# Softmax sums spread by two 64-column products, twelve key rows throughout, and two head pairs prepared between projections

## The chip, the cores and the metric

The kernel runs on one core of one Trainium2 chip. The metric is device time in microseconds (us); the kernel before takes 3126.86 us, the median of three runs (3126.22 to 3132.38). Less is better.

## What is computed

A two-layer backbone works on 1024 latent tokens (a grid of 16 rows by 64 columns) and 256 context tokens, 1024 channels wide, in float32. Each layer has a modulated norm, one input projection that feeds three parallel mixers (mLSTM, neighbourhood attention, RG-LRU), an output projection with a gated residual, and an MLP. The change touches the attention mixer of 8 heads of 64 channels:

```python
q, k = rmsnorm(q.reshape(sh), qn_g), rmsnorm(k.reshape(sh), kn_g)
...
s_loc = einsum('bqhd,brqchd->bhqrc', q_r, k_win) * scale      # a window of 8 rows x 16 columns of keys
s_loc = s_loc + bias                                          # relative-position table
s_ctx = einsum('bqhd,bkhd->bhqk', q_r, kc) * scale            # 256 context keys
p = softmax(concatenate([s_loc, s_ctx], axis=-1), axis=-1)
o = einsum(p_loc, v_win) + einsum(p_ctx, vc)
```

In the first layer the 256 context queries attend to the context as well; in the last layer they are left out.

## The kernel before, in words

**Precision.** Weights and activations are split into two float32r parts, so that each projection is three TensorE products (L436, L451, L1325, L1477). Score products use stacks [hi; lo] of q against [hi; hi] and [lo; lo] of k.

**Order.** The program is written as one trace; a list scheduler orders each engine's in-order queue by a simulated timeline and, among what is ready there, by the order in the program. So an instruction that stands late in the program can be put early when the simulation has its inputs and its buffer ready, and a queue then waits at that place until they really are.

**Stages around the change, in each layer.** `na_group(0)` and `na_group(1)` (L610) project k, q and v of heads 0 to 3 and 4 to 7, token tile by token tile (`proj_tm`, 24 products a tile in alternating PSUM banks p and q), and spill them to DRAM. `na_prep(hp)` (L625) prepares one pair of heads from that spill in 6 steps (5 in the last layer): load `ut` (L642), scale by the norm on VectorE (L645), transpose up to 4 tiles on TensorE (L653, L655), split into hi and lo on ScalarE and VectorE (L661, L662, L666, L667), copy across partitions by DMA (L669, L672, L673). Pairs 0 and 1 need only group 0. Before, pair 0 is written after `na_group(1)` (L1285), and pair hp+1 step by step inside the attention of pair hp, through `side()` (L1373). `side()` also issues steps of the output projection (`fill`, L1345), whose product bank is one bank p with an evacuation on VectorE (L1342). In layer 0 the projections also share TensorE with pending modulation steps (L266, L274), which load 512 KB of weights each.

**Attention of a pair** (`na_att`, L726). A unit is 8 rows x 16 columns of queries of both heads: 8 latent units a pair, and 2 context units a pair in layer 0 (72 units in all). Scores go to bank a (L795 for the window, L799 for the context), VectorE adds the table `tab` and takes the minimum (L809, L813), ScalarE exponentiates and sums into `den` (L816). `softmax_pv` (L676) transposes the scores (L688), copies them to SBUF (`PT`: L690, L705 on ScalarE, L707 on VectorE), inverts `den` (L710), copies it out to 64 columns a head (`rb`, L712), transposes that (L714) into the upper half of bank c, and multiplies by the values (L718) into the lower half. `yd` then copies and scales the result (L826, L827). Units of query group g = 0 use 11 key rows (352 keys, so that the third key tile has 96), those of g = 1 use 12. The tables of a column tile are loaded (L769) and get one GpSimd addition of a prepared mask tile `crm` (L772). `crm` is made once a layer (L1368, L1371).

**Memory.** The pool `ns` (stacks, `ut`, `ql`) opens before `na_group(1)` in space that the mLSTM leaves; the pool `na_` (npl: scores, `PT`, `rb`, `VC`, `tab`, `VB`, `crm`) opens after it, when the normalised input is closed.

Of the kernel before, what the change touches and what calls it, by code (L numbers as in the profile page):

```python
# [21 lines left out]
P = 128  # L22
# [11 lines left out]
# column offsets inside the combined input projection  # L34
# [4 lines left out]
# token blocks: (offset, size, is_context)  # L39
# [3 lines left out]
def host_consts():  # L43
    """Arrays that depend on shapes alone."""
# [19 lines left out]
    # column mask: partitions (h, ic'), [3 column types, 32 key columns]  # L64
# [8 lines left out]
    # row mask: partitions (i', ic'), [group slot (1, 0), 12 key rows]  # L73
# [18 lines left out]
def backbone_kernel(ctx: ExitStack, tc: tile.TileContext, I, out, dbg=None):  # L92
# [9 lines left out]
    # the normalised blocks lie on one side, all else on the other; they change sides after each attention  # L102
# [62 lines left out]
    def rsqrt(x, tmp_i, tmp_z, y):  # L165
        """y = 1/sqrt(x) for positive x, to float32 accuracy (integer seed and Newton steps)."""
# [7 lines left out]
    def rsqrt_mean(ss, n, inv, tag):  # L174
        """1/sqrt(ss * inv + EPS) of a [P, n] tile of sums."""
# [29 lines left out]
    def w_fm(w, l, c0, r0=0, kt=KT, cols=P):  # L205
        """Weight tile [P, kt, cols] of rows r0.. and columns c0.. of layer l."""
# [41 lines left out]
    # c_act, cctx_act: 32 columns per k tile (two used)  # L248
# [69 lines left out]
    def mod_sum(l, j, ns):  # L318
        """Sums over the partitions of the products of ns steps."""
# [1237 lines left out]
```

## Time and profile before

| | |
|---|---|
| three runs, us | 3132.38, 3126.86, 3126.22 |
| span of the profiled execution, us | 3122.6 |
| PE busy | 3016.5 us, 97% of the span |
| DVE busy | 1898.7 us, 61% |
| ACT busy | 1129.1 us, 36% |
| POOL busy | 288.9 us, 9% |
| mean granted TensorE clock, of 2.4 GHz | 0.989 |

The span runs from the first to the last instruction of one execution taken by the profiler; the page prints no other time of that execution. The three runs lie 3.6 to 9.8 us above the span. PE is TensorE's products, PEld its weight loads, DVE VectorE, ACT ScalarE, POOL GpSimd, SP the queue that issues most transfers. A busy PE is not a PE at its peak, since ends of products are modelled. The granted clock has two levels, 1.2 and 2.4 GHz; a window's figure is the mean share of 2.4 GHz.

### The profile page before, as it was taken

Reading aid. Unit: us, or ns where it says so; the run is one execution under the profiler, and the core shown is the slowest. Engines: PE = TensorE matmul, PEld = TensorE weight load, DVE = VectorE, ACT = ScalarE, POOL = GpSimd, SP = SyncE. Lnnn points to the kernel's source line nnn. Section 1 sums busy time; section 2 is a strip of 40 time slices with the busy share of each in tenths; the row PEclk is TensorE's granted clock in tenths of the full one; section 3 lists DMA queues with packets and bytes.
Section 4 is the critical chain, followed back from the end, with each engine's and each line's share of the span. In section 5 each row is a group of like instructions: output and inputs, shape, how many; then the busy total and the mean of one; then the engine's idle time right before and its main releaser. Section 6 shows DMA issues by size and latency. Waiting matters only on the chain.

```text
span 3122.6 us, 47473 instructions
## 1 busy us (share of the span) xinstructions
PE 3016.5 (97%) x18250; PEld 2553.0 (82%) x18250; DVE 1898.7 (61%) x4318; ACT 1129.1 (36%) x2011; POOL 288.9 (9%) x252
## 2 busy tenths in 40 slices
PE   7999998999899999999999999998899999999999
PEld 6888887878788888887778889997787777887877
DVE  5757654887887666455444584755787444444444
ACT  4632223674422222233222453234564223332222
POOL 0410010122200000010000511002222000000000
PEclk9999999999899999999999999999999999999999
DMA  9624667865233444233333532348753332343333
GB/s 272 223 73 124 174 172 206 234 186 176 67 109 109 123 127 124 79 108 99 92 94 95 176 122 82 101 123 222 223 169 113 95 95 88 99 117 90 93 96 93
DMA packets 531098, 410.73 MB, mean 132 GB/s; under 512 B 27580, under 2 KB 496536, under 8 KB 530872
## 3 DMA queue, kind: packets, MB, share of 16 engines
q1 hardware_dynamic: 519448, 387.41, 42.1%
q0 software_dynamic: 8576, 15.00, 1.5%
q10 hardware_dynamic: 2848, 5.28, 0.6%
q8 instruction: 144, 2.36, 0.3%
q14 instruction: 82, 0.67, 0.1%
HBM read 339.72 MB, written 67.53 MB: 130 GB/s over the span
## 4 chain that ended last, share of the span: by engine, by line
PE 70%; DVE 11%; DMA 10%; issue 2%; ACT 2%; SPq 1%; POOL 0%; ACTq 0%; DVEq 0%; POOLq 0%
PE psa L436 15%; PE psa L1477 14%; PE psq L436 5%; PE psp L436 5%; PE psp L1477 5%; PE psq L1477 5%; PE psp L451 4%; DMA mr<-in_w_mod_dram 4%; PE psq L451 4%; PE psp L1325 2%; DVE ma L312 2%; PE psc L718 2%; DVE wl L201 1%; PE psa L1325 1%; PE psb L688 1%
## 5 line engine op out<-in xcount | busy, mean ns | idle before, releaser
L200 ACT ACTIVATE wh<-wr 128x1024 fp32r<-128x1024 f32 (+3 forms) x356 | 361.6, 1021 | 946.5 <-PE psa L1477 307.3
L201 DVE TENSOR_TENSOR wl<-wr,wh 128x1024 fp32r<-128x1024 f32 (+3 forms) x356 | 425.0, 1198 | 386.4 <-ACT wh L200 380.0
L436 PE MATMUL psa<-xlo,wh 128*128 128x512 f32 (+1 forms) x856 | 319.7, 374 | 2.2 <-DVE xlo L412 2.2
L436 PE MATMUL psa<-xh,wh 128*128 128x512 f32 (+1 forms) x856 | 319.4, 373 | 2.4 <-ACT xh L411 2.3
L436 PE MATMUL psa<-xh,wl 128*128 128x512 f32 (+1 forms) x856 | 319.6, 373 | 1.4 <-DVE wl L201 1.4
L1477 PE MATMUL psa<-hl,wh 128*128 128x512 f32 (+1 forms) x768 | 286.0, 373 | 0.6 <-DVE hl L211 0.6
L1477 PE MATMUL psa<-hh,wh 128*128 128x512 f32 (+1 forms) x768 | 284.2, 375 | 0.3 <-ACT wh L200 0.3
L1477 PE MATMUL psa<-hh,wl 128*128 128x512 f32 (+1 forms) x768 | 277.9, 373 | 0.6 <-DVE wl L201 0.6
L1481 DVE SCALAR_TENSOR_TENSOR res<-psa,modt,res 128x512 f32<-128x512 f32 (+1 forms) x192 | 131.0, 693 | 170.3 <-PE psa L1477 169.9
L436 PEld LDWEIGHTS psa<-xh,wh 128*128 128x128 f32 x856 | 162.1, 190 | 33.4 <-ACT xh L411 3.1
L436 PEld LDWEIGHTS psa<-xlo,wh 128*128 128x128 f32 x856 | 162.1, 189 | 33.1 <-DVE xlo L412 2.6
L436 PEld LDWEIGHTS psa<-xh,wl 128*128 128x128 f32 x856 | 162.1, 189 | 32.3 <-DVE wl L201 2.2
L377 POOL TENSOR_TENSOR acc<-acc,nsq 128x512 f32<-128x512 f32 (+1 forms) x56 | 77.9, 1401 | 1026.9 <-ACT nsq L376 976.5
L1477 PEld LDWEIGHTS psa<-hh,wh 128*128 128x128 f32 x768 | 144.3, 188 | 34.6 <-ACT wh L200 8.6
L451 PE MATMUL psp<-wl,xh 128*128 128x256 f32 (+1 forms) x560 | 164.0, 293 | 4.3 <-DVE wl L201 4.2
L1477 PEld LDWEIGHTS psa<-hh,wl 128*128 128x128 f32 x768 | 144.3, 188 | 28.7 <-DVE wl L201 1.5
L1477 PEld LDWEIGHTS psa<-hl,wh 128*128 128x128 f32 x768 | 144.4, 188 | 27.4 <-DVE hl L211 0.8
L210 ACT ACTIVATE hh<-rl 128x512 fp32r<-128x512 f32 (+1 forms) x160 | 93.5, 589 | 202.1 <-DVE rl L1453 202.0
L451 PE MATMUL psp<-wh,xh 128*128 128x256 f32 (+1 forms) x560 | 161.9, 289 | 2.4 <-ACT wh L200 2.4
L451 PE MATMUL psq<-wh,xh 128*128 128x256 f32 (+1 forms) x560 | 161.7, 289 | 1.4 <-ACT usq L605 0.9
L451 PE MATMUL psq<-wl,xh 128*128 128x256 f32 (+1 forms) x560 | 160.6, 287 | 0.0
L451 PE MATMUL psp<-wh,xlo 128*128 128x256 f32 (+1 forms) x560 | 159.9, 286 | 0.0
(409 smaller groups left out, 7328.5 us busy)
## 6 DMA issues: line engine op xcount, KB each, us to landing
wr<-in_w_mlp_dram SPq DMA_DIRECT2D x256, 512.0 KB
mr<-in_w_mod_dram SPq DMA_DIRECT2D x92, 512.0 KB
wr<-in_w_in_dram SPq DMA_DIRECT2D x48, 512.0 KB
tab<-T_d SPq DMA_DIRECT2D x48, 384.0 KB
T_d<-E_d POOLq DMA_DIRECT2D x48, 256.0 KB, 6.6
ab<-row_d SPq DMA_DIRECT2D x36, 256.0 KB
xT_d<-res SPq DMA_DIRECT2D x4, 2048.0 KB
wr<-in_w_out_dram SPq DMA_DIRECT2D x32, 256.0 KB
```

What stands on the lines that cost most here:

```text
L200: act.activation(hi[:, a:b], raw[:, a:b], AF.Copy)
L201: dve.tensor_sub(lo[:, a:b], raw[:, a:b], hi[:, a:b].bitcast(F32))
L210: act.activation(hi, src32, AF.Copy)
L312: dve.scalar_tensor_tensor(a, raw[:, k], s[:, k], a, op0=OP.mult, op1=OP.add)
L377: pool.tensor_add(acc[bi], acc[bi], sq[:, :n])
L436: m = pe.matmul(t[:, :n], w[a][:, k, :], X[bi][b][:, k, :], start=(i == 0), stop=(i == 23))
L451: pe.matmul(t[:, :cols], X[bi][b][:, half * 4 + k, o:o + P], ws[half][a][:, k, :], start=(i == 0), stop=(i == 23))
L688: pe.transpose(t[:w, j * P:(j + 1) * P], S[e][:, o:o + w], permT)
L718: pe.matmul(to[64 * e:64 * e + 64, :P], vals[i][:w, 64 * e:64 * e + 64], PT[:w, e, i], start=(i == 0), stop=(i == nt - 1))
L1325: pe.matmul(t[:, :n], w[a][:, k, cc * P:(cc + 1) * P], Y[bi][b][:, k], start=(i == 0), stop=(i == 11))
L1477: m = pe.matmul(t[:, :n], w[a][:, k, cc * P:(cc + 1) * P], H[bi, k][b], start=(i == 0), stop=(i == 3 * GH - 1))
L1481: dve.scalar_tensor_tensor(xr[bi][:, ct], t[:, :n], G2[:, ct, v:v + 1], xr[bi][:, ct], op0=OP.mult, op1=OP.add)
```

## The change

`softmax_pv` no longer copies `den` to 64 columns and transposes it; for each head one product takes `den` itself, read 64 times, as a 64-column stationary operand against the permutation. All units use 12 key rows, so all key tiles have 128 keys and `PT` is copied in whole pieces. `crm` is dropped: each table gets two GpSimd additions with masks read repeatedly. `VC` and `tab` move from pool npl to `ns`. Steps of the first two pairs' preparation are written after every second token tile of `na_group(1)`, until 12 (10 in the last layer) have been issued, and both are completed there; `side()` prepares only pairs 2 and 3, beside the attention of pairs 1 and 2. What else the diff changes is comments.

```diff
-        def na_proj(grp, c0, dst, toks, stat):
+        def na_proj(grp, c0, dst, toks, stat, side):
...
+                if side is not None:
+                    side()
             proj_tm(ws, 256, X, toks, ev)
...
-                    t = bank("b" if hp < 1 else "bbq")
+                    t = bank("b" if hp < 2 else "bbq")
...
-                    o, w = tiles[i]
-                    pe.transpose(t[:w, j * P:(j + 1) * P], S[e][:, o:o + w], permT)
+                    pe.transpose(t[:, j * P:(j + 1) * P], S[e][:, tiles[i]:tiles[i] + P], permT)
...
-                while j < 4:
...
-                    if e == 0:
-                        act.activation(PT[:w, e, j:j2], src, AF.Copy)
-                    else:
-                        dve.tensor_copy(PT[:w, e, j:j2], src)
-                    j = j2
+                elif gi == 0:
+                    act.activation(PT[:, 0, 0:4], t.rearrange("p (k q) -> p k q", q=P), AF.Copy)
+                else:
+                    dve.tensor_copy(PT[:, 1, 0:4], t.rearrange("p (k q) -> p k q", q=P))
             dve.reciprocal(den, den)
-            rb_ = npl.tile([P, 2, 64], F32, name=nm("rb"), tag="rb", bufs=2)
-            dve.tensor_copy(rb_, den.unsqueeze(2).to_broadcast([P, 2, 64]))
             to = bank("c")
-            pe.transpose(to[:, P:2 * P], rb_.rearrange("p e d -> p (e d)"), permT)
+            for e in range(2):
+                pe.matmul(to[64 * e:64 * e + 64, P:2 * P], den[:, e:e + 1].to_broadcast([P, 64]), permT,
+                          start=True, stop=True)
...
-            VC = npl.tile([P, 2, P], F32, name=nm("VC"), tag="VC", bufs=1)
+            VC = ns.tile([P, 2, P], F32, name=nm("VC"), tag="VC", bufs=1)
...
-                    tb_ = npl.tile([P, 2, 384], F32, name=nm("tab"), tag="tab", bufs=4)
+                    tb_ = ns.tile([P, 2, 384], F32, name=nm("tab"), tag="tab", bufs=4)
...
-                    pool.tensor_add(tv, tv, crm[ct].rearrange("p (r c) -> p r c", c=32))
+                    pool.tensor_add(tv, tv, masks[:, 96:120].unsqueeze(2).to_broadcast([P, 24, 32]))
+                    pool.tensor_add(tv, tv, colm[:, None, ct, :].to_broadcast([P, 24, 32]))
...
-                        nr = 11 if g == 0 else 12
+                        nr = 12
...
+        steps = [p_ for hp in range(2) for p_ in [preps[hp]] * (5 if last else 6)]
+        done = [0]
+        def prep_step():
+            done[0] += 1
+            if done[0] % 2 == 0 and steps:
+                phase(f"na_prep{l}")
+                next(steps.pop(0), None)
+                phase(f"na_inB{l}")
         phase(f"na_inB{l}")
-        na_group(1)
+        na_group(1, prep_step)
         phase(f"na_prep{l}")
-        for hp in range(1):
+        for hp in range(2):
             run(preps[hp])
...
-            crm = [npl.tile([P, 768], F32, name=nm("crm"), tag="crm", bufs=3) for _ in range(3)]
...
-                    if 0 <= hp < 3:
-                        for _ in range(1):
-                            next(preps[hp + 1], None)
+                    if 1 <= hp < 3:
+                        next(preps[hp + 1], None)
```

## Rows read from the trace of the kernel before

**Rows 1.** Windows, layer 0 attention: length; PE, PEld, DVE, ACT, POOL; clock; DMA.

```profile
515.70:588.00 72.30, 61.78 (x452) 52.14 (x453) 55.05 (x157) 38.96 (x93) 14.54 (x8) 0.95 0.84 232
588.00:690.00 102.00, 96.12 (x821) 80.88 (x818) 87.16 (x285) 71.75 (x187) 24.50 (x13) 0.98 0.73 207
690.00:748.00 58.00, 58.00 (x488) 49.94 (x488) 39.28 (x138) 32.31 (x89) 5.48 (x3) 1.00 0.50 162
```

**Rows 2.** Windows, layer 1 attention; DMA is a share, then GB/s.

```profile
2131.50:2192.00 60.50, 51.73 (x322) 41.36 (x321) 43.43 (x108) 30.47 (x68) 22.05 (x12) 0.94 0.95 251
2192.00:2292.00 100.00, 90.87 (x736) 73.85 (x735) 79.11 (x249) 60.17 (x154) 22.79 (x12) 0.97 0.78 217
2292.00:2349.00 57.00, 55.25 (x495) 46.88 (x494) 42.47 (x149) 35.59 (x96) 10.85 (x6) 1.00 0.53 170
```

**Rows 3.** PE's waits in 515 to 745 us: waiter, releaser, total us, times, longest.

```profile
PE psa L741 <- issue: 2.4, 1, 2.4
PE psc L714 <- DVE nmx L750: 2.2, 1, 2.2
```

**Rows 4.** PE's waits in 2133 to 2347 us.

```profile
PE psa L795 <- DVE m L809: 3.9, 4, 2.3
...
PE psp L1325 <- DVE xs L1342: 2.8, 1, 2.8
PE psa L795 <- DMA QS<-ql: 2.4, 1, 2.4
```

**Rows 5.** Timeline of DVE: start, us, instruction, idle time before it and releaser.

```profile
539.80 0.63 DVE L645 TENSOR_TENSOR ut<-ut,rsn 128x256 f32<-128x256 f32 x1 [2.57 <-DMA ut<-u_nq]
```

**Rows 6.** DVE's groups, 515 to 746 us: busy us, mean ns; idle before, releasers.

```profile
L809 DVE CUSTOM_DVE_ANT_0 S<-psa,tab 128x384 f32<-128x384 f32 x32 | 17.1, 550 | 2.8 <-PE psa L795 2.7
L809 DVE CUSTOM_DVE_ANT_0 S<-psa,tab 128x352 f32<-128x352 f32 x32 | 16.0, 515 | 0.9 <-PE psb L688 0.5 <-issue 0.4
L712 DVE COPY rb<-den 128x128 f32<-128x128 f32 x40 | 14.9, 372 | 1.3 <-PE psc L714 0.7
...
L645 DVE TENSOR_TENSOR ut<-ut,rsn 128x512 f32<-128x512 f32 x13 | 8.9, 688 | 11.7 <-DMA ut<-u_nq 8.6 <-DMA ut<-u_nk 3.1
...
L707 DVE COPY PT<-psb 128x512 f32<-128x512 f32 x12 | 8.3, 689 | 2.9 <-PE psb L688 1.7 <-PE psc L718 1.2
...
L707 DVE COPY PT<-psb 128x256 f32<-128x256 f32 x12 | 5.1, 422 | 2.1 <-PE psc L718 2.1
...
L707 DVE COPY PT<-psb 128x128 f32<-128x128 f32 x12 | 3.3, 277 | 0.0
```

**Rows 7.** Timeline of PE in one unit: start, us, instruction.

```profile
643.77 0.60 PE L688 MATMUL psq<-idj,S 128*128 128x128 f32 x4
...
644.44 0.27 PE L714 MATMUL psc<-idj,rb 128*128 128x128 f32 x1
644.64 0.88 PE L718 MATMUL psc<-PT,VB 128*64 128x128 f32 x12
```

**Rows 8.** PE's groups, 515 to 746 us: the window's scores.

```profile
L795 PE MATMUL psa<-KH,QS 128*128 128x384 f32 x32 | 13.2, 412 | 0.0
...
L795 PE MATMUL psa<-KH,QS 128*128 128x352 f32 x32 | 12.7, 397 | 0.0
```

**Rows 9.** Source L772 over the span: ns min/median/max, first and last start.

```profile
L772 POOL TENSOR_TENSOR tab<-tab,crm x48: 1799/1831/2892, 526.8 to 2310.8; 128x768 f32<-128x768 f32 x48
```

**Rows 10.** Source L1371 over the span, columns as before.

```profile
L1371 POOL TENSOR_TENSOR crm<-crm,masks x6: 1805/2054/2821, 442.2 to 2139.8; 128x768 f32<-128x768 f32 x6
```

**Rows 11.** Source L645 over the span, columns as before.

```profile
L645 DVE TENSOR_TENSOR ut<-ut,rsn x44: 406/691/1670, 454.7 to 2281.8; 128x512 f32<-128x512 f32 x32, 128x256 f32<-128x256 f32 x12
```

**Rows 12.** Windows of the second group's projections, from the first preparation load on.

```profile
451.00:515.70 64.70, 59.67 (x565) 56.69 (x564) 21.00 (x60) 16.92 (x42) 0.00 (x0) 0.95 0.69 187
...
2097.00:2131.50 34.50, 33.20 (x277) 32.42 (x277) 13.40 (x42) 12.41 (x28) 0.00 (x0) 1.00 0.54 172
```

**Rows 13.** PE's longest wait in 478 to 503 us.

```profile
PE psc L274 <- DMA mr<-in_w_mod_dram: 5.0, 1, 5.0
```

More of the change, by code (lines that the diff above doesn't have):

```diff
@@ L607, in ev, with na_group @@
                                       axis=AX.X, op=OP.add)
+                if side is not None:
+                    side()
             proj_tm(ws, 256, X, toks, ev)
-        def na_group(grp):
-            na_proj(grp, C_NK, u_nk[l], ALLT, nssq["k"])
-            na_proj(grp, C_NQ, u_nq[l], QT, nssq["q"])
-            na_proj(grp, C_NV, u_nv[l], ALLT, None)
+        def na_group(grp, side=None):
+            na_proj(grp, C_NK, u_nk[l], ALLT, nssq["k"], side)
+            na_proj(grp, C_NQ, u_nq[l], QT, nssq["q"], side)
+            na_proj(grp, C_NV, u_nv[l], ALLT, None, side)
             for kd, toks in (("q", QT), ("k", ALLT)):
@@ L686, in softmax_pv @@
                 for j, (e, i) in enumerate(gr):
-                    o, w = tiles[i]
-                    pe.transpose(t[:w, j * P:(j + 1) * P], S[e][:, o:o + w], permT)
+                    pe.transpose(t[:, j * P:(j + 1) * P], S[e][:, tiles[i]:tiles[i] + P], permT)
                 if len(gr) == 2:
                     act.activation(PT[:, :, 4], t[:, 0:2 * P].rearrange("p (k q) -> p k q", q=P), AF.Copy)
-                    continue
-                if nt == 2:
+                elif nt == 2:
                     act.activation(PT[:, :, 0:2], t.rearrange("p (e k q) -> p e k q", e=2, q=P), AF.Copy)
-                    continue
-                e = gi
-                j = 0
-                while j < 4:
-                    j2 = j
-                    w = tiles[j][1]
-                    while j2 < 4 and tiles[j2][1] == w:
-                        j2 += 1
-                    src = t[:w, j * P:j2 * P].rearrange("p (k q) -> p k q", q=P)
-                    if e == 0:
-                        act.activation(PT[:w, e, j:j2], src, AF.Copy)
-                    else:
-                        dve.tensor_copy(PT[:w, e, j:j2], src)
-                    j = j2
+                elif gi == 0:
+                    act.activation(PT[:, 0, 0:4], t.rearrange("p (k q) -> p k q", q=P), AF.Copy)
+                else:
+                    dve.tensor_copy(PT[:, 1, 0:4], t.rearrange("p (k q) -> p k q", q=P))
             dve.reciprocal(den, den)
-            rb_ = npl.tile([P, 2, 64], F32, name=nm("rb"), tag="rb", bufs=2)
-            dve.tensor_copy(rb_, den.unsqueeze(2).to_broadcast([P, 2, 64]))
             to = bank("c")
-            pe.transpose(to[:, P:2 * P], rb_.rearrange("p e d -> p (e d)"), permT)
+            for e in range(2):
+                pe.matmul(to[64 * e:64 * e + 64, P:2 * P], den[:, e:e + 1].to_broadcast([P, 64]), permT,
+                          start=True, stop=True)
             for i in range(nt):
-                w = tiles[i][1]
                 for e in range(2):
-                    pe.matmul(to[64 * e:64 * e + 64, :P], vals[i][:w, 64 * e:64 * e + 64], PT[:w, e, i],
+                    pe.matmul(to[64 * e:64 * e + 64, :P], vals[i][:, 64 * e:64 * e + 64], PT[:, e, i],
                               start=(i == 0), stop=(i == nt - 1))
@@ L818, in na_att @@
                             S.append(s_)
-                        tiles = [(i * P, min(P, nl - i * P)) for i in range(3)] + [(nl, P), (nl + P, P)]
+                        tiles = [i * P for i in range(5)]
                         vals = [VB[:, i + g] for i in range(3)] + [VC[:, 0], VC[:, 1]]
@@ L1363, in due @@
                 return (i + 1) * pace[key] // n_side - i * pace[key] // n_side
-            crm = [npl.tile([P, 768], F32, name=nm("crm"), tag="crm", bufs=3) for _ in range(3)]
-            for ct in range(3):
-                pool.tensor_copy(crm[ct].rearrange("p (r c) -> p r c", c=32),
-                                 masks[:, 96:120].unsqueeze(2).to_broadcast([P, 24, 32]))
-                cv_ = crm[ct].rearrange("p (r c) -> p r c", c=32)
-                pool.tensor_add(cv_, cv_, colm[:, None, ct, :].to_broadcast([P, 24, 32]))
             for hp in range(4):
```

2 lines of the change are left out of this document (1 added, 1 removed).

## The prediction

> **What bounds the kernel now.** The first page's totals come first: TensorE (PE) is busy for 97% of the span, so a gain can only come from PE's idle time, from stretches at the lower clock, or from less PE work. Next come windows over the two attention stages, cut where the head pairs begin. In layer 0 the stretch of pair 0 lasts 72.3 us with PE busy for 61.8 at a granted clock of 0.95; the last pair's 58.0 us have no idle time and the full clock [rows 1]. Layer 1 looks alike: 60.5 us with 51.7 busy at 0.94 for pair 0, and 57.0 with 55.3 at the full clock for pair 3 [rows 2]. What differs is the preparation: beside pair 0 the end of pair 0's own and all of pair 1's runs, beside pair 3 none. Counting idle time, and busy time times the clock's shortfall, as loss, the first stretches lose 10.5 + 3.1 = 13.6 us and 8.8 + 3.1 = 11.9, the two middle pairs 5.9 + 1.9 = 7.8 and 9.1 + 2.7 = 11.8, the last pairs 0 and 1.8. That is 46.9 us in both layers, the most that the attention could give back without losing work.
>
> The list of PE's waits then names the holders. In layer 0 the two longest are 2.4 us before the first scores, put down to "issue" while the last cross-partition copies of pair 0's stacks are under way, and 2.2 us for VectorE (DVE) [rows 3]. DVE itself stood still for 2.57 us just before, behind one preparation instruction, the scaling at L645, which waited for its load [rows 5]. In layer 1 it is 2.4 us for the stacks' copy, 2.8 for an evacuation on DVE and 3.9 for score banks that DVE had not read [rows 4]. In the groups of layer 0 L645 has 11.7 us of such standing before its 13 longer calls [rows 6]. So it is less PE's own length than the preparation in DVE's in-order queue.
>
> **The change, part by part.** *Preparation of pairs 0 and 1 between the projections.* PE's work in it only moves: 20 transposes a pair at 0.11 us ((0.60 - 0.27)/3 from the four transposes and the one product in the unit shown [rows 7]) are 2.2 us, later or earlier, and cost nothing net. What moves with them off the first stretch are DVE's L645 and its waits, the splits, and the loads and copies on SyncE's queue, which pass the spill stores of the projections and, in layer 0, the modulation loads. At least the named waits should go: 2.4 + 2.2 + 2.4 + 2.8 = 9.8 us. At most the first stretch comes to look like the last, which gives 25.5 less a start of about 2 us a layer, an estimate from the chain of one unit, where one DVE minimum is 0.5 us [rows 6] and four steps follow: 21. I take 15, the middle, since the scores still can't be written before the input's space is free, and the filling output projection keeps its one bank.
>
> The price stands in the projections. A pair's preparation moves 1.31 MB of loads, 0.66 MB for QS and 1.31 MB for KH and KL, 3.3 MB by the code's shapes; at 232 GB/s for a share of 0.84 [rows 1], thus 276 at the full share, that is 12 us. In layer 0 the 64.7 us from the first preparation load to the end of the projections have a DMA share of 0.69 [rows 12], some 20 us free; pair 1 and the rest of pair 0 (4 us, guessed as a third) take 16. In layer 1 34.5 us at 0.54 leave 16 us free for the same 16. Both fit, barely. When they don't, the next thing late in layer 0 is a modulation step: PE waited 5.0 us for its weights once already [rows 13], and that window's clock of 0.95 over 64.7 us says that 3.2 us were lost besides: 8.2 us an event. The steps' own transposes queue in the same place. Bounds: none and two such events, 0 to 16; I take 5, nearer to none, as layer 1 has no such loads.
>
> *Sum spreading.* DVE loses L712: 40 calls and 14.9 us in layer 0, with a mean of 372 ns [rows 6]. On PE one transpose gives way to two 64-column products, of the form that L718 already has: twelve take 0.88 us with one tail of 0.27, 0.055 each, so the pair costs 0.11 like the transpose. The first product after the transpose started 0.20 us behind it, not 0.11 [rows 7]: 0.09 us go where the array turns from 128 to 64 columns. That turn comes once a unit, before or after the change, as long as the pair stands right before the value products: 0 us, with 72 x 0.09 = 6.5 us as the upper end if it stands apart and the array turns once more, and 0 as the lower. The Trainium skill, "TensorEngine Tiling (Array Packing)", Key Properties, says that a change of tiling mode drains the engine; by that rule a pair that stands apart pays, and the 0.20 us agree.
>
> *Twelve rows.* A score product of 384 keys is 15 ns longer than one of 352 (412 against 397 [rows 8]); four a unit in 32 units are 1.9 us on PE, which nothing hides. DVE pays 35 ns twice (550 against 515) and saves 422 + 277 + 277 - 689 = 287 ns on the third copy pattern, the 96-key piece taken like the 128-key one [rows 6]; ScalarE loses the same two copies. With L712, DVE sheds 14.9 + 4.6 - 1.1 = 18.4 of its 181.5 us in layer 0 [rows 1, 6]. In the middle pairs, where preparation stays, that should soften waits. Their loss is 19.6 us in all; between 0 and half of it, I take 5, a quarter.
>
> *Masks.* `crm` leaves GpSimd, and each of 48 tables gets a second addition; the like one with a repeated mask took 2.05 us in the median [rows 10] beside 1.83 for the present one [rows 9]. None of the waits of [rows 3, 4] is for a table, so the addition lies beside other work; SyncE loads tables ahead, and DVE, ScalarE and PE would queue behind a late one. It can hold DVE another way: L645 took 0.69 us in the median and 1.67 at most [rows 11], and 12 remain in the attention of a layer, at most 0.98 each. I take 1 us on the path, from 0 to 4. The Trainium skill, "SBUF — State Buffer", Who interferes with whom, says that a DVE instruction with two SBUF inputs contends with a GpSimd instruction that reads SBUF and that the loser blocks; it speaks against the second addition, and the maximum agrees. The tables' and values' new place lets the first tables of a layer load early; it is inside the first term.
>
> **Sum.** -15 + 5 (projections) + 0 (spreading) + 1.9 - 5 + 1 = -12.1 us. The span 3122.6 becomes 3110.5; the runs' median lies 4.3 above the profiled span, so 3126.9 becomes 3114.8, and I say 3115.
>
> **The rivals.** *More than that:* the first stretches really turn into copies of the last and the middle pairs get half of their loss back: -21 - 10 + 1.9 = -29, 3098 us. For it speaks that pair 3 without preparation loses nothing in layer 0; against it that pair 3 begins with its banks full and the first pair empty.
>
> *The start is late anyway:* with the stacks ready, the chain from scores to values still waits for space and for DVE behind the weight splits of the output projection, and PE idles there as now. Then only 5 of the 15 are left: -5 + 5 + 1.9 - 5 + 1 = -2, 3125 us. For it: 2.8 us of layer 1 were an evacuation, not a preparation [rows 4].
>
> *The projections pay:* DMA in layer 0's second group is full, loads for the 12 steps and for the modulation come later than planned, and PE's in-order queue stops at the transposes and at the modulation products. At 8.2 us an event, with the rest of the sum at -17, the third event turns the sign; four give +16, 3143 us. For it: the share of 0.69 before anything is added, and the 5.0 us there now [rows 12, 13]. Against it: the scheduler also places the loads earlier.
>
> *The spread doesn't fuse:* the pair is put among the 128-column products, and 6.5 us go to additional turns: -12.1 + 6.5 = -5.6, 3121 us.
>
> **How the numbers follow.** Forecast 0.50, more 0.15, late start 0.17, projections pay 0.13, turns 0.05. The range takes the bounds of the forecast's terms: -21 + 0 - 10 + 1.9 = -29 below, and -9.8 + 16 + 1.9 + 1 = +9 above: 3098 to 3136; it leaves out the last rival and the tails. A measurement can tell 0.2%, 6.3 us, from no change: faster is under 3120.6, slower over 3133.1. Of the forecast 0.44 lies under 3120.6 and 0.06 beside it; with "more" and a part of the late start that gives 0.63 faster; the rest of the late start, the turns and small stalls give 0.22 the same; the projections' rival and its tail 0.15 slower.
>
> **What would show it.** Right: pair 0's stretches of [rows 1, 2] with PE idle under 5 us and the full clock, no wait of a first score for QS, no DVE standing before L645 beside pair 0; L712 gone; the first value product still 0.20 us behind what comes before the spread; projections no longer than before plus 2 to 5 us. Wrong: longer waits for `mr` or `ut` between the projections, a score step that waits for `tab`, idle time at the start under new names, or middle pairs that lose more than 19.6 us because preparation now meets them alone.

## The result, and the profile after

The changed kernel takes 3153.19 us (median of 4 runs, 3148.36 to 3154.8) against 3127.8 for the kernel before beside it (3126.22 to 3132.38): a ratio of 1.0081, 95% interval [1.0067, 1.0095]. It is slower by about 25 us, and the forecast of 3115 (3098 to 3136) was wrong in its sign. In a later comparison (run w_again, the same kernel) the ratio is 1.0071 [1.0056, 1.0086].

The profiled execution has a span of 3146.5 us, 23.9 more than before. First its totals: busy time and share of the span, and behind x the instructions.

```profile
span 3146.5 us, 47740 instructions
PE 3033.9 (96%) x18466; PEld 2570.4 (82%) x18466; DVE 1890.4 (60%) x4182; ACT 1131.1 (36%) x1947; POOL 339.4 (11%) x288
```

DVE and ACT have fewer instructions, as meant. PE has 216 more records than before's 18250, three for each of the 72 units, and POOL 50.5 us more work. PE is idle for 112.6 us in place of 106.1, so of the 23.9 us only 6.5 are idle time; its busy time is 17.4 us longer, by new work and by a mean granted clock of 0.986 in place of 0.989.

The windows answer rows 1, 2 and 12 (length; PE, PEld, DVE, ACT, POOL; clock; DMA share, GB/s). Of after, first the attention of layer 0, then of layer 1, cut where the head pairs begin, and then four whole stages: the second group's projections of layer 0, the output projection behind its attention, and the same two of layer 1.

```profile
531.10:580.00 48.90, 46.11 (x388) 39.52 (x388) 32.94 (x105) 26.58 (x64) 13.99 (x8) 0.97 0.56 170
580.00:705.00 125.00, 112.33 (x942) 94.38 (x942) 90.25 (x257) 74.56 (x177) 42.83 (x25) 0.95 0.68 188
705.00:760.50 55.50, 54.77 (x497) 46.43 (x495) 33.53 (x110) 29.84 (x72) 13.76 (x8) 1.00 0.42 137
...
2158.60:2199.00 40.40, 34.18 (x224) 26.87 (x225) 24.27 (x69) 17.47 (x37) 6.50 (x4) 0.96 0.76 223
2199.00:2307.00 108.00, 105.07 (x863) 87.57 (x862) 80.82 (x228) 65.78 (x144) 40.55 (x24) 0.97 0.74 210
2307.00:2356.10 49.10, 47.02 (x489) 40.85 (x487) 32.25 (x118) 30.67 (x79) 19.54 (x12) 1.00 0.43 135
```

```profile
390.90:531.10 140.20, 125.61 (x1138) 118.23 (x1137) 78.70 (x220) 43.46 (x98) 14.05 (x8) 0.93 0.74 205
760.50:829.30 68.80, 60.31 (x298) 50.11 (x299) 51.02 (x109) 27.03 (x46) 22.13 (x19) 0.93 0.46 147
2044.90:2158.60 113.70, 104.05 (x849) 100.69 (x848) 73.73 (x190) 40.07 (x91) 14.28 (x8) 0.98 0.58 165
2356.10:2409.40 53.30, 47.88 (x203) 38.15 (x202) 33.69 (x49) 23.08 (x34) 19.31 (x13) 0.97 0.39 129
```

The same four stages in the kernel before:

```profile
390.20:515.90 125.70, 115.76 (x1100) 109.02 (x1100) 62.12 (x192) 32.96 (x81) 9.70 (x6) 0.96 0.64 179
754.40:807.40 53.00, 49.12 (x228) 40.38 (x229) 45.62 (x96) 22.82 (x38) 26.70 (x19) 0.94 0.44 134
2028.30:2131.60 103.30, 99.57 (x819) 97.14 (x818) 51.61 (x170) 32.01 (x76) 0.09 (x1) 0.98 0.43 132
2347.60:2386.60 39.00, 37.99 (x165) 30.02 (x166) 28.70 (x42) 18.74 (x27) 19.80 (x13) 1.00 0.33 102
```

Loss is counted as in the prediction: idle time, and busy time times the clock's shortfall.

| stretch, both layers | loss before, us | loss after, us | difference |
|---|---|---|---|
| first pair's attention | 25.5 | 4.2 + 7.6 = 11.8 | -13.7 |
| other pairs' attention | 21.4 | 18.3 + 0.7 + 6.1 + 2.1 = 27.2 | +5.8 |
| second group's projections | 14.6 + 5.7 = 20.3 | 23.4 + 11.7 = 35.1 | +14.8 |
| output projection behind the attention | 6.8 + 1.0 = 7.8 | 12.7 + 6.9 = 19.6 | +11.8 |

The differences add up to +18.7. With 7.6 us of new PE work (below) and 1.9 for the rows that is 28.2, against a span longer by 23.9; the stages outside the table were 3.5 us shorter. The first two rows of the table are not quite like for like: in after, the first scores of pair 0 in layer 0 start at 490.0 us, between the projections, and the work that fills gaps lies elsewhere (388 PE records beside the first pair, 452 before; 942 beside the middle pairs, 821 before).

### The profile page after: what moved, and what is told of

The parts are those of the page before. It is cut to its first block, busy times and chain, and to the rows that moved or that the text cites. A ratio compares the mean times of both kernels' runs of the same rounds, so it can differ in the third digit from the quotient of the medians.

```text
span 3146.5 us, 47740 instructions
## 1 busy us (share of the span) xinstructions
PE 3033.9 (96%) x18466; PEld 2570.4 (82%) x18466; DVE 1890.4 (60%) x4182; ACT 1131.1 (36%) x1947; POOL 339.4 (11%) x288
## 4 chain that ended last, share of the span: by engine, by line
PE 66%; DVE 6%; DMA 4%; ACT 1%; issue 1%; SPq 0%; ACTq 0%; DVEq 0%
PE psa L436 15%; PE psa L1471 14%; PE psq L436 5%; PE psp L436 5%; PE psp L1471 5%; PE psq L1471 5%; PE psp L1327 2%; PE psp L451 2%; PE psq L451 2%; PE psc L706 1%; DMA mr<-in_w_mod_dram 1%; PE psa L1327 1%; DVE ma L312 1%; PE psb L689 1%; PE psa L786 1%
## 5 line engine op out<-in xcount | busy, mean ns | idle before, releaser
L210 ACT ACTIVATE hh<-rl 128x512 fp32r<-128x512 f32 (+1 forms) x160 | 93.6, 589 | 222.0 <-DVE rl L1447 222.0
L451 PE MATMUL psq<-wh,xlo 128*128 128x256 f32 (+1 forms) x560 | 161.8, 289 | 0.0
```

What stands on the lines that cost most here:

```text
L210: act.activation(hi, src32, AF.Copy)
L451: pe.matmul(t[:, :cols], X[bi][b][:, half * 4 + k, o:o + P], ws[half][a][:, k, :], start=(i == 0), stop=(i == 23))
```

## How far one execution can be read

The kernel before was profiled again (b_again), and a kernel with the same instructions in another order was made (n_heads). The edit of n_heads, in the value products:

```diff
-                for e in range(2):
+                for e in (1, 0):
                     pe.matmul(to[64 * e:64 * e + 64, :P], vals[i][:w, 64 * e:64 * e + 64], PT[:w, e, i],
```

> The kernel before once more, for a second profile. If stages of a few us can be read from one execution, every stage stays within 3 us of the first profile. If the first profile was a lucky one, attention and projections of layer 0 are 4 to 6 us longer, as in the profiles of the reordered kernel and of twelve rows.

> The kernel before with the value products of the second head written ahead of those of the first in each key tile: the same instructions, nothing added or taken away. It gives the size of what a new order alone does. Theory (prices of 6 us and more in the parts are prices of the parts): within 3 us of the kernel before. Rival (any edit reshuffles the queues by 5 us or more): 5 us or more off, either way, with stages that lengthen and shorten against each other.

The second execution of before has a span of 3130.1 us, 7.5 longer than the first, and no stage of the table below is more than 3.7 off. Over 20 runs on one chip before ranged from 3123.18 to 3143.54. The reordered kernel took 3135.25 us against 3131.55, a ratio of 1.0008 [0.9990, 1.0025], while its profiled execution has a layer-0 attention 5.4 us longer. So this new order is worth nothing that the runs can tell, the theory's side, but a stage of one execution is only good to about 5 us, the rival's. The +10 and more of the projections and the output projection stand clear of that.

The table below has the stage lengths of one execution of each kernel, less those of the first profile of before (in us; stages from the first product of the second group's projections on), and the ratio of the timed runs to before's on the same chip. The kernels not described yet follow.

| kernel | proj. L0 | att. L0 | out. L0 | proj. L1 | att. L1 | out. L1 | ratio, 95% interval |
|---|---|---|---|---|---|---|---|
| b_again | -2.4 | +0.2 | +0.3 | +0.6 | +3.7 | -0.1 | |
| n_heads | +3.0 | +5.4 | 0.0 | -1.1 | +2.4 | -0.1 | 1.0008 [0.9990, 1.0025] |
| a_rows | +1.9 | +4.7 | -3.4 | -2.1 | -0.8 | 0.0 | 0.9999 [0.9984, 1.0013] |
| p_act12 | +4.0 | +4.7 | +0.2 | -2.6 | +6.3 | -0.1 | 1.0012 [1.0000, 1.0024] |
| a_spread | +0.6 | +4.8 | +0.8 | -0.4 | +8.4 | -1.2 | 1.0051 [1.0036, 1.0066] |
| s_double | +0.5 | +17.2 | -0.4 | -4.5 | +4.0 | -1.1 | 1.0036 [1.0024, 1.0047] |
| a_masks | +4.0 | -4.1 | +15.9 | -1.9 | -7.3 | +16.8 | 1.0033 [1.0021, 1.0045] |
| m_place | +2.5 | -0.3 | +16.1 | -0.3 | -3.6 | +13.9 | 1.0063 [1.0042, 1.0084] |
| c1_pool | +6.0 | +10.4 | -1.9 | -4.8 | +1.8 | -0.1 | 1.0021 [1.0007, 1.0036] |
| m_adds | -0.5 | +8.9 | -1.9 | -2.2 | +15.5 | -0.1 | 1.0048 [1.0028, 1.0068] |
| a_inter | +10.9 | +0.4 | -1.7 | +5.5 | -8.2 | -0.1 | 1.0020 [1.0007, 1.0032] |
| i_l1 | +3.4 | +0.6 | -0.1 | +6.6 | -4.5 | -0.1 | 1.0006 [0.9994, 1.0019] |
| u_spread | +13.0 | -10.7 | +17.3 | +15.9 | -20.1 | +12.9 | 1.0061 [1.0044, 1.0077] |
| u_masks | +14.6 | +4.9 | -2.0 | +7.1 | +1.4 | -0.1 | 1.0054 [1.0035, 1.0072] |
| u_inter | +3.3 | +1.7 | +16.4 | -3.2 | +8.6 | +12.5 | 1.0108 [1.0093, 1.0123] |
| after | +14.4 | -9.1 | +15.8 | +10.4 | -18.5 | +14.3 | 1.0081 [1.0067, 1.0095] |
| w_again | +13.3 | -8.3 | +16.5 | +12.9 | -16.6 | +13.5 | 1.0071 [1.0056, 1.0086] |

## Each part alone

Four kernels have one part of the change each: a_spread the two products, a_inter the steps between the projections, a_masks the two additions with `VC` and `tab` in `ns`, a_rows the twelve rows. Their edits are the hunks of the change shown above; the core of each:

```diff
a_spread:
-            dve.tensor_copy(rb_, den.unsqueeze(2).to_broadcast([P, 2, 64]))
-            pe.transpose(to[:, P:2 * P], rb_.rearrange("p e d -> p (e d)"), permT)
+            for e in range(2):
+                pe.matmul(to[64 * e:64 * e + 64, P:2 * P], den[:, e:e + 1].to_broadcast([P, 64]), permT,
a_inter:
-        na_group(1)
+        na_group(1, prep_step)
a_masks:
-            VC = npl.tile([P, 2, P], F32, name=nm("VC"), tag="VC", bufs=1)
+            VC = ns.tile([P, 2, P], F32, name=nm("VC"), tag="VC", bufs=1)
-                    pool.tensor_add(tv, tv, crm[ct].rearrange("p (r c) -> p r c", c=32))
+                    pool.tensor_add(tv, tv, masks[:, 96:120].unsqueeze(2).to_broadcast([P, 24, 32]))
+                    pool.tensor_add(tv, tv, colm[:, None, ct, :].to_broadcast([P, 24, 32]))
a_rows:
-                        nr = 11 if g == 0 else 12
+                        nr = 12
```

> The kernel before with the two 64-column products in place of the copy and the transpose, and nothing else. Theory S (the spread is dear: the trace of the changed kernel shows four product records a unit, not two, 0.27 us from the first to the first value product where the transpose had 0.20, and the array's turn now ahead of them): +0.1 to 0.16 us in each of 72 units, 3134 to 3139 us. Theory P (the preparation alone lost the time): within 4 us of before, or a few us faster for the 26 us of copies that VectorE sheds.

> The kernel before with the preparation of pairs 0 and 1 written between the second group's projections, and nothing else: copy and transpose, 11 or 12 rows, prepared masks and their pool as before. Theory P (the interleaved steps stop TensorE's queue in the projections): 3140 to 3150 us, the projections of layer 0 and 1 10 us longer each. Theory M (the tables' additions that moved forward do the harm, by holding VectorE): 3115 to 3127 us, the forecast of the prediction for this term.

> The kernel before with two GpSimd additions a table in place of the prepared masks, and with VC and tab in the earlier pool, and nothing else. Theory M: the first four tables of a layer load and add between the projections, and preparation there is late: +3 to +10 us. Theory P: within 3 us of before, since the additions lie beside other work.

> The kernel before with 12 key rows in all units and whole copies of the transposed scores, and nothing else. Prediction's term: +1.9 us on TensorE, against copies shorter by 0.29 us on VectorE and 0.33 on ScalarE in 32 units: 3122 to 3130 us under every theory.

Against 3133.44 for before, a_spread took 3148.51 us, a_inter 3140.01, a_masks 3143.94 and a_rows 3132.54. Three parts cost time on their own, 15, 6.6 and 10.5 us; the rows cost nothing that can be measured. No part gains. a_inter lies at the lower end of theory P; a_spread and a_masks lie above what any theory had for them.

**The spread has a price on PE.** One unit of after, from PE's timeline (start, us, instruction):

```profile
648.15 0.44 PE L702 MATMUL psc<-idj,den 128*64 128x128 f32 x4
648.42 0.82 PE L706 MATMUL psc<-PT,VB 128*64 128x128 f32 x12
649.08 0.61 PE L706 MATMUL psc<-PT,VC 128*64 128x128 f32 x8
```

Two float32 products of 64 columns are four records, where the transpose was one [rows 7]. The twelve records of the value products of [rows 7] say so already: three key tiles and two heads are six products. Take the units in which PE didn't stand still ahead of the spread (65 of before, 59 of after). The time from the end of the product ahead of it to the first value product rose in the median from 0.039 to 0.198 us, and the 20 value records took 1.192 in place of 1.246. That is +0.105 us a unit, and for 72 units 7.6; a_spread gives 0.198 and 1.195, thus 0.108 and 7.8. The remaining half of a_spread's 15 us has no line of its own. s_double was to size it, by doing the pair of products twice:

```diff
             for e in range(2):
                 pe.matmul(to[64 * e:64 * e + 64, P:2 * P], den[:, e:e + 1].to_broadcast([P, 64]), permT,
                           start=True, stop=True)
+            for e in range(2):
+                pe.matmul(to[64 * e:64 * e + 64, P:2 * P], den[:, e:e + 1].to_broadcast([P, 64]), permT,
+                          start=True, stop=True)
```

> The kernel before with the two products done twice over, each time into the same place: measures the price of the pair. Theory S (a product of float32 is two records, the pair 0.22 us on TensorE and nothing hides it): 72 x 0.22 = 16 us over the kernel with one pair, so about 3164 us where that had 3148. If the attention has slack that hides part of TensorE's work: +5 us or less over it.

It took 3144.23 us against 3133.57, so 10.7 over before and not above a_spread. Its layer-0 attention is 17.2 longer, but the projections of layer 1 came out 4.5 shorter. On PE the second pair costs just what theory S said: 0.417 us from the product ahead to the first value product where a_spread has 0.198, thus 0.219 a unit and 15.8 in 72. Yet the kernel is no slower for it. So PE's price of the pair is shown, but not that the kernel pays it in full: the four records account for at most 7.8 of a_spread's 15 us, and the rest stays open.

**A lighter DVE gives nothing.** The copy to 64 columns went to ScalarE, with twelve rows, and the transpose stayed:

```diff
-            dve.tensor_copy(rb_, den.unsqueeze(2).to_broadcast([P, 2, 64]))
+            act.activation(rb_, den.unsqueeze(2).to_broadcast([P, 2, 64]), AF.Copy)
```

> The kernel before with twelve rows, and with the copy of the sums to 64 columns on ScalarE in place of VectorE; the transpose stays. So VectorE sheds the same 15 us a layer that the change takes from it, and TensorE pays nothing for it. The prediction's step (a lighter VectorE softens the middle pairs, -5, against +1.9 for the rows): 3 to 6 us under the kernel before, and a version faster than both kernels. Rival (VectorE is not what ends PE's waits there): within 3 us of the kernel with twelve rows alone, which was equal to the kernel before.

It took 3136.81 us against 3131.55, a ratio of 1.0012 [1.0000, 1.0024]: no gain, the rival's side. It isn't relief alone, since ScalarE is busy for 8.5 and 6.5 us more in the two attentions. In a_spread no engine takes the copy over, and PE's waits for DVE in the attentions are no shorter there either, 13.5 and 17.6 us in all (before 9.6 and 14.1, b_again 12.4 and 17.9). So what DVE sheds in the change was not what held PE in the attention of before.

## The masks: where the tables lie, and the second addition

Three kernels take a_masks apart. m_place moves `VC` and `tab` to `ns` and keeps `crm`; c1_pool puts the two in a pool of their own, opened after `ns`; m_adds makes the two additions with both in npl.

```diff
m_place:
-                    tb_ = npl.tile([P, 2, 384], F32, name=nm("tab"), tag="tab", bufs=4)
+                    tb_ = ns.tile([P, 2, 384], F32, name=nm("tab"), tag="tab", bufs=4)
c1_pool:
+        nt_cm = tc.tile_pool(name=f"nt_{l}", bufs=1, reuse_waits="tile")
+        nt = nt_cm.__enter__()
-                    tb_ = npl.tile([P, 2, 384], F32, name=nm("tab"), tag="tab", bufs=4)
+                    tb_ = nt.tile([P, 2, 384], F32, name=nm("tab"), tag="tab", bufs=4)
m_adds:
-                    pool.tensor_add(tv, tv, crm[ct].rearrange("p (r c) -> p r c", c=32))
+                    pool.tensor_add(tv, tv, masks[:, 96:120].unsqueeze(2).to_broadcast([P, 24, 32]))
+                    pool.tensor_add(tv, tv, colm[:, None, ct, :].to_broadcast([P, 24, 32]))
```

> The kernel before with VC and tab in the pool ns, and nothing else: prepared masks and one addition a table. Theory L (lifetime: the normalised input of the output projection lies on ns's space, and with VC and tab there it can't be written before the attention ends): the stage after the attention 10 to 16 us longer in each layer, part of it given back before; +7 to +12 us in all. Theory M (the second addition is what costs): within 3 us of before.

> As m_place, but VC and tab in a pool of their own that opens right after ns, so above it. Theory L: the first blocks of the next input no longer wait, the stage after the attention is as before, and the time is within 4 us of before or up to 6 us faster, as tables load early. A rival to L (early tables harm by their loads and additions alone): +5 to +12 us as in m_place.

> The kernel before with two GpSimd additions a table in place of prepared masks, VC and tab in npl as before. Theory M: +5 to +10 us, from VectorE held by GpSimd. Theory L: 0 to +3 us, and no longer stage after the attention.

The place alone costs 20 us (3153.64 against 3133.57), the own pool 6 (3139.8). In the table the output projections of m_place are 16.1 and 13.9 us longer, those of c1_pool as short as before's. What is late is ScalarE's split of the mixers' result, the first input of the output projection. Source L210 (ns min/median/max, first and last start) of before, c1_pool, m_place and after:

```profile
L210 ACT ACTIVATE xh<-yl x9: 408/624/642, 732.7 to 756.1; 128x512 fp32r<-128x512 f32 x6, 128x256 fp32r<-128x256 f32 x3
```

```profile
L210 ACT ACTIVATE xh<-yl x9: 412/623/642, 749.9 to 773.3; 128x512 fp32r<-128x512 f32 x6, 128x256 fp32r<-128x256 f32 x3
```

```profile
L210 ACT ACTIVATE xh<-yl x9: 408/621/635, 760.8 to 778.6; 128x512 fp32r<-128x512 f32 x6, 128x256 fp32r<-128x256 f32 x3
```

```profile
L210 ACT ACTIVATE xh<-yl x9: 407/622/635, 760.7 to 778.2; 128x512 fp32r<-128x512 f32 x6, 128x256 fp32r<-128x256 f32 x3
```

Before starts them 21.7 us ahead of the end of its last value product (754.4 us), and so does c1_pool (771.6). m_place and after start them 0.2 us behind it (760.6 and 760.5). By the order in which the pools open, the tiles of the next stage lie in these two where `VC` and `tab` lie, and so wait for the last table and the last context values; c1_pool differs from m_place in that place alone and has no such delay. PE then waits; after, from 755 to 830 us (waiter, releaser: total us, times, longest):

```profile
PE psa L1327 <- ACT xh L210: 8.5, 2, 7.8
```

In m_place the same wait is 8.8 us with a longest of 8.1, and neither c1_pool nor before has it. Some of the longer output projection is work that filled gaps inside the attention before (228 records of PE there, 298 now, and an attention shorter by 9.1), so the price is the sum of both stages: +15.8 and +10.3 in m_place. c1_pool's own 6 us lie outside theory L (within 4 us of before, or faster) and at the lower end of its rival: early tables seem to cost something by themselves, which no run here shows alone.

The second addition has its own price: m_adds costs 16 us (3149.47), all of it in the attention. In layer 1 PE's waits for DVE there add up to 27.1 us, against 14.1 before and 17.9 in b_again. The two largest entries:

```profile
PE psp L1326 <- DVE xs L1343: 8.3, 5, 4.9
PE psa L800 <- DVE m L814: 5.6, 3, 5.1
```

Before has 2.8 and 3.1 us for the same two, b_again 6.5 and 4.2. What the second addition holds on DVE is above all one instruction, the copy of `den` to 64 columns (L712). Its group over the whole span (busy us, mean ns), in before and in m_adds:

```profile
L712 DVE COPY rb<-den 128x128 f32<-128x128 f32 x72 | 26.3, 365 | 4.8 <-PE psc L714 3.3
```

```profile
L712 DVE COPY rb<-den 128x128 f32<-128x128 f32 x72 | 38.0, 528 | 5.9 <-PE psc L714 4.8
```

In the median the copy takes 0.22 us in both. None that has no GpSimd instruction beside it takes more than 0.23, but the longest take 1.77 and 1.84 us; 12 of the 72 in before and 28 in m_adds take over 0.3, and each of these runs beside a GpSimd instruction. So GpSimd holds this copy for 10.2 us before (72 x 0.142) and for 21.7 in m_adds (72 x 0.301). That this is what costs the 16 us is not shown: p_act12, where DVE has no such copy, gained nothing. In the changed kernel the copy is gone, so the price of m_adds doesn't carry over to the whole.

Place and addition together (a_masks, 10.5) cost less than either; why they soften each other wasn't settled.

## The early preparation, alone and inside the change

i_l1 is the kernel before with the early preparation in the last layer only, where no modulation weights are loaded:

```diff
-            if done[0] % 2 == 0 and steps:
+            if last and done[0] % 2 == 0 and steps:
```

> The kernel before with the first two pairs prepared between the projections in the last layer alone, where no modulation weights are loaded. Theory (there the projections pay 5 us and the attention gives back 8, as in the profile of the early preparation alone; layer 0, where loads collide, holds its loss): 0 to 5 us under the kernel before, a version at or ahead of both. Rival (the projections pay as much wherever it is done): 3 to 8 us over it.

It took 3134.37 us against 3134.78, a ratio of 1.0006 [0.9994, 1.0019], so it's no faster. In layer 1 the projections are 6.6 us longer and the attention 4.5 shorter: layer 1 pays as well, without modulation loads. In a_inter, layer 0 pays 10.9 and its attention gives nothing back, since the start stays late for other reasons. PE's waits there, 528 to 580 us, and the first 40 us of both attentions:

```profile
PE psp L1338 <- DVE xs L1355: 6.3, 2, 3.7
PE psp L1338 <- ACT wh L200: 1.7, 1, 1.7
```

```profile
528.20:567.50 39.30, 30.98 (x179) 26.08 (x179) 18.82 (x57) 13.80 (x33) 10.90 (x6) 0.83 0.75 220
2152.00:2192.00 40.00, 27.52 (x142) 21.70 (x141) 22.13 (x53) 11.83 (x26) 21.23 (x12) 0.91 0.92 263
```

PE is idle for 8.3 and 12.5 us of these, now mostly behind an evacuation of the output projection (8.2 us in layer 1) and its weights.

Then parts were taken out of the whole: u_spread has the copy and the transpose back, u_masks `crm` and the places in npl, u_inter the old preparation, all else as in the changed kernel. Their edits are the hunks above, reversed:

```diff
u_spread:
+            dve.tensor_copy(rb_, den.unsqueeze(2).to_broadcast([P, 2, 64]))
+            pe.transpose(to[:, P:2 * P], rb_.rearrange("p e d -> p (e d)"), permT)
u_masks:
+            VC = npl.tile([P, 2, P], F32, name=nm("VC"), tag="VC", bufs=1)
+                    pool.tensor_add(tv, tv, crm[ct].rearrange("p (r c) -> p r c", c=32))
u_inter:
-        na_group(1, prep_step)
+        na_group(1)
```

> The changed kernel with the sums spread as before (copy on VectorE, one transpose); twelve rows, masks and early preparation stay. Theory (a pair of float32 products is four passes, 0.108 us more a unit on TensorE in 72 units, and the rest of the 15 us of that part alone comes from it): the whole change's 25 us over the kernel before shrink to 10 to 17. Rival (the parts' prices are mostly reordering by the scheduler and don't add): anything from 15 to 30 us over the kernel before, with the gain not tied to the spread.

> The changed kernel with crm, one addition a table and VC and tab in the pool npl as before; spread, twelve rows and early preparation stay. Theory (VC and tab in ns lie under the next stage's input, so its first splits wait for the end of the attention): the stretch from the last value product to the end of the output projection is 14 us shorter than in the changed kernel in each layer, some of it given back inside the attention, and the time is 7 to 12 us less. Rival (the preparation between the projections is held by the tables' additions, not by its own loads): the second group's projections also lose their 10 to 14 us a layer and the time is 20 us or more less.

> The changed kernel with the preparation of the first two pairs as before; spread, twelve rows, two additions and the space in ns stay. Theory (the whole pays in the projections, 25 us in both layers, and the preparation beside the attention costs about 10 of those back): 10 to 15 us over the kernel before, with the second group's projections back to within 4 us of it. Rival (the parts alone add up): 24 us over it, as spread and masks alone cost 15 and 10.

> The changed kernel once more, timed beside the same runs of the kernel before as the kernel without the early preparation. 20 to 25 us over the kernel before; in its profile the second group's projections are again 10 us or more longer in each layer than in the kernel before, and the stretch from the last value product to the end of the output projection 14 us or more. If those were one execution's chance, they are within 5 us.

u_spread took 3154.65 us and u_masks 3152.66, both against 3131.55 for before; u_inter took 3165.93 and w_again 3155.82, both against 3134.78. The parts don't add up: alone they cost 31 together and the whole costs 21 to 25. w_again came out as expected (21 us over before, projections and output projections longer as in the first profile). Taking out the spread or the masks saves 3 to 9 us by the ratios, 1.0061 and 1.0054 against 1.0071 and 1.0081, whose intervals overlap. The theory on the spread fails there: 10 to 17 us over before was expected, 23 came by the medians and 19 by the ratio. u_masks has its output projections back to before's length, as the theory on the space wants, but its attentions are 14.0 and 19.9 us longer than after's, so nothing is left of that gain: inside the whole, the price of the place doesn't show. Taking out the early preparation makes it 10 us *slower*, against both the theory and its rival: inside this change the early preparation is a gain. None of the three parts, taken out by itself, brings back the time of before, so which part costs the whole its 21 to 25 us stays open; the stages in which it is lost are the ones of the table.

The trace of u_inter shows what the early preparation gains there. Its projections are back to before's length, but in its attentions PE's waits for DVE add up to 22.0 and 26.8 us, against 11.2 and 10.2 in after. Many of them are for the preparation, which writes `ut` and `KL` (layer 0, 520 to 760 us, then layer 1):

```profile
PE psc L701 <- DVE yr L815: 6.2, 2, 5.5
PE psb L655 <- DVE KL L662: 4.9, 2, 3.5
PE psq L655 <- DVE ut L645: 3.6, 1, 3.6
```

```profile
PE psc L705 <- DVE PT L695: 4.7, 1, 4.7
PE psq L687 <- DVE KL L662: 3.6, 1, 3.6
PE psb L653 <- DVE KL L662: 3.0, 1, 3.0
```

In the table its two attentions are 10.8 and 27.1 us longer than after's; with the output projections, which differ by +0.6 and -1.8, that is 36.7. Moving pair 1's preparation away gives them back, and the projections take 11.1 + 13.6 = 24.7 of them: -12 by the stages and -10 by the timed runs. Where the attention has less to lose, alone, the same move gives 9.6 against 16.4 paid, and the timed runs cost 6.6.

**What the projections pay.** Of +14.4 in layer 0 after, idle time is 4.7 (14.6 against 9.9), the clock's shortfall 4.2 (0.93 against 0.96) and 38 more records, 28 moved transposes and 10 products of the first scores, 4.2 at 0.11 us each. Of +10.4 in layer 1 idle time is 5.9 (9.6 against 3.7), 30 more records, 28 of them transposes, are 3.3, and the clock is 0.98 in both. PE's waits in layer 0's projections, before (390 to 516) and after (391 to 531):

```profile
PE psc L274 <- DMA mr<-in_w_mod_dram: 8.4, 4, 5.0
```

```profile
PE psc L274 <- DMA mr<-in_w_mod_dram: 12.3, 7, 4.0
```

In layer 1, 2100 to 2162 us, PE's queue stops at the preparation's transposes instead. The profile names no releaser for most of that ("issue"), but the two timelines (DVE, then POOL) show one: the transposes start at 2124.13 and 2129.57 us, each 0.1 us behind the end of an L647.

```profile
PE psb L655 <- issue: 5.5, 3, 3.8
PE psb L657 <- DVE ql L669: 1.5, 1, 1.5
```

```profile
2122.06 1.97 DVE L647 TENSOR_TENSOR ut<-ut,rsn 128x512 f32<-128x512 f32 x1
2124.06 0.69 DVE L664 TENSOR_TENSOR KL<-psb,KH 64x512 fp32r<-64x512 f32 x1
2124.79 2.44 DVE L172 SCALAR_TENSOR_TENSOR rsn<-sz,rsn 128x32 f32<-128x32 f32 x2
2127.15 2.33 DVE L647 TENSOR_TENSOR ut<-ut,rsn 128x512 f32<-128x512 f32 x1
```

```profile
2120.07 1.91 POOL L762 TENSOR_TENSOR tab<-tab,masks 128x768 f32<-128x768 f32 x1
2121.94 1.54 POOL L761 TENSOR_TENSOR tab<-tab,masks 128x768 f32<-128x768 f32 x1
2123.44 2.28 POOL L762 TENSOR_TENSOR tab<-tab,masks 128x768 f32<-128x768 f32 x1
2125.68 1.48 POOL L761 TENSOR_TENSOR tab<-tab,masks 128x768 f32<-128x768 f32 x1
2127.12 4.03 POOL L762 TENSOR_TENSOR tab<-tab,masks 128x768 f32<-128x768 f32 x2
```

The tables come early, since their place in `ns` is free early, and eight GpSimd additions stand back to back from 2116.87 to 2131.15, just where the preparation now runs. The scaling L647, like L645 before [rows 11] at 0.69 us in the median over the span, takes 1.97 and 2.33 beside them. The split L664, with one input in PSUM, keeps its 0.69. The Trainium skill, "SBUF — State Buffer", Who interferes with whom, has DVE share a pair of SBUF ports with GpSimd under an exclusive lock; the difference between L647 and L664 agrees. u_masks has no such additions there and pays 7.1 in layer 1's projections (a_inter 5.5, i_l1 6.6). u_inter and a_masks have the additions without the preparation and pay nothing (-3.2 and -1.9). Only both together reach 10.4 to 15.9.

## Why the prediction was wrong, point by point

The sum went wrong in its prices, not in its gain. The first stretches gave 13.7 us of the 15 forecast. But the projections' term of +5 measured +14.8 in loss alone, spreading at 0 measured 7.6 of work on PE, the middle pairs' -5 became a loss, and the output projection behind the attention, +11.8, has no term in the sum at all.

**What bounds the kernel:** the reading of the first stretches was right. Their loss fell by 13.7 us, where the sum had -15, and PE's waits of [rows 3, 4] for the stacks are gone from the start. From 531 to 580 us after has this left:

```profile
PE psp L1327 <- ACT wh L200: 2.5, 1, 2.5
```

In layer 1 the evacuation [rows 4] is what stayed, 5.4 us up to 2200 us.

**Projections, +5:** the mis-sized half of the first term. The loss there rose by 14.8, inside the bounds (0 to 16) but three times the value taken, and another 7.5 us of work moved in, transposes above all. The bounds were built from modulation loads, and the value was taken near nothing because layer 1 has none; yet layer 1 paid 5.5 to 7.1 us without the early additions and 10.4 to 15.9 with them, the rest through DVE and GpSimd, a mechanism that the prediction priced only inside the attention. The rival *the projections pay* had the place right, but its events of 8.2 us did not come: the waits for modulation weights grew from 8.4 to 12.3 us, none longer than 4.0. The net of the term, -10, is what w_again and u_inter measure inside the change (-10), but that is luck: it is made of -36.7 and +24.7.

**Spreading, 0:** the price per product was taken from twelve records as if they were twelve products; they are six. The pair costs four records, not two, and 0.105 us more a unit, 7.6 in all, above the prediction's own upper end of 6.5 us. The turn of the array was looked at instead of the number of records. The Trainium skill, "TensorEngine Tiling (Array Packing)", Restrictions, says that column tiling rules out the transpose mode for float32; no run here asks for a transpose of 64 columns, and the rows only show one record for the full transpose and two for each 64-column product.

**Twelve rows, +1.9:** no difference was measured (a_rows, 0.9999), as far as 1.9 can be told.

**Middle pairs, -5:** wrong. Their loss rose from 19.6 to 24.4 us, which the prediction had named as a sign of being wrong, and neither p_act12 nor a_spread gained by a relief of DVE.

**Masks, +1:** the largest failure. The new place was looked at from one side only, when the tables can load, not from the other, when their space can be given back. Alone (m_place) it costs 20 us; inside the whole the loss in the output projections is 11.8, though undoing place and additions there gains only 5 to 9. The bound of 4 us for the second addition counted L645 alone and in the attention alone. In before the copy L712 met GpSimd more, and the 14.9 us that [rows 6] have for it are in good part waiting. The change takes it away, so the 16 us of m_adds are no measure of this term; what the additions cost inside the whole is in the projections of layer 1.

**The rivals:** *the start is late anyway* holds in a_inter, with the evacuation on DVE that it named. *More* and *the spread doesn't fuse* did not come; in 64 of 72 units (71 before) the value products directly follow the pair.

## What to carry to other kernels

When a tile changes its pool, ask what opens in that space next and when it could start before: a tile that lives until the end of a stage takes away the overlap with the next stage; alone, that made the next stage 14 to 16 us longer a layer here, and the kernel 20 us slower. A mean well above the median in a group of rows is a sign that something holds the instruction: look for what runs beside it. Count matmul records in the trace against the products in the code before taking a price per product, float32 above all. A step moved out of a crowded stage is worth what that stage loses to it and costs what the receiving stage loses, and both depend on what else shares the engine there: the same move was worth -10 us with the other parts in place and +7 without them.

## What the runs showed of the hardware

A GpSimd addition of a mask with each element read 32 times in a row (L761) took 1.48 us in the median, less than the 1.83 of one with a dense mask [rows 9] or with a repeated row of 32 (L762):

```profile
L761 POOL TENSOR_TENSOR tab<-tab,masks x48: 1469/1482/2538, 463.8 to 2325.8; 128x768 f32<-128x768 f32 x48
L762 POOL TENSOR_TENSOR tab<-tab,masks x48: 1804/1828/2827, 466.7 to 2327.4; 128x768 f32<-128x768 f32 x48
```

The prediction had 2.05 for the second addition, from the one that made `crm` [rows 10]. So the additions' length was not what the prediction took too low; what they hold on DVE was (L647 up to 2.33 us in place of 0.69). In before, the copy L712 is held in the same way, up to 1.77 us in place of 0.22.
